# A decoder layer on one core: x over two other queues, its squares behind the operands, low halves on POOL, idle products, two more accumulator banks

## The chip, the core and the metric

The kernel runs on one core of one Trainium2 chip. A core has five engines with a queue each: TensorE (PE in the profile), VectorE (DVE), ScalarE (ACT), GpSimd (POOL) and SyncE (SP), which only issues loads. Loads and stores can be issued from SP, ACT and POOL. Each engine runs its queue strictly in order, and waits on semaphores for the others. The metric is the device time of one execution in microseconds (us), the median of the runs.

## The reference

One layer of a hybrid decoder for a prompt of 512 positions and a sample group of 8 x 8 positions, 576 columns in all, which share the weights. Only its start matters here:

```python
def rmsnorm(x, w):
    xf = x.astype(jnp.float32)
    y = xf * lax.rsqrt(jnp.mean(xf * xf, axis=-1, keepdims=True) + RMS_EPS)
    return (y * w.astype(jnp.float32)).astype(x.dtype)

def swiglu(x, w_gate, w_up, w_down):
    return (jax.nn.silu(x @ w_gate) * (x @ w_up)) @ w_down

def trunk_layer(x, conv_prev, h0, past, p):
    h = x + 0.5 * swiglu(rmsnorm(x, p['ffn1_norm']), p['ffn1_w_gate'], p['ffn1_w_up'], p['ffn1_w_down'])
    ...
```

Behind this first feed-forward step come the combined input projection, the Mamba-2 scan, attention over a paged cache with summed log forget values (cache_logf), the projections and a second feed-forward step. D_MODEL is 1024, D_FF 2816.

## The kernel before

Activations lie transposed: eight tiles hts[k] of 128 features x 576 columns. A float32 product is made of three products in float32r: both operands are split into a high half and a low half (names with hi or h, lo or l), and mm3 adds hi x hi, hi x lo and lo x hi in one PSUM bank. One accumulator holds 128 outputs x 288 columns, so each 128 outputs of a weight matrix take two accumulators (half 0 and 1) of 8 x 3 = 24 products.

At the start (from L352 on) x is loaded in five tiles xin of 128 rows, two halves each, and transposed by TensorE (tr for the prompt, mm for the sample). Norm.add makes xh on ScalarE and xl on VectorE. Weights come in stages of 512 KB (stage, L161), are copied to whi by ScalarE (L173) and the rest goes to wlo by VectorE, or POOL in a later part of the kernel (L174); whi and wlo have four buffers each. The row scales of the norm are not needed by the products: ScalarE squares the rows of xin with a sum into x0 (rsx, L391), VectorE takes the inverse root in 13 small steps, and spread (L243, L249) multiplies it out on TensorE into rbc. Only the instructions that empty an accumulator (g at L327, u at L337, both VectorE) need rbc. So TensorE can run ahead by as many accumulators as there are free banks: the tags acc and pv have two banks each.

The first feed-forward step takes for each 128 hidden features f first the gate, then the up matrix: g, its tanh on ScalarE (th, L296), s on VectorE (L297), u on VectorE, the product u times s on POOL (L338), hh on ScalarE and hl on POOL.

Beside this the setup runs: parameter loads (r, L402 to L411, transposed at L413), the page table (pcol), the convolution state (sc, transposed by TensorE at L460, copied to scT by VectorE, stored to scD), and the forget values of the cache: a gather on POOL (lg, L469), 16 scans on VectorE (pf, L474), a total (tot), one small product with the matrix page on TensorE (mm_388, L480; called the page product below), its copy st, 16 subtractions on POOL (L485) and 32 stores to pastD from ScalarE's queue (L491).

The order within each queue is set when the program is built: a scheduler replays the code with its own costs and fixes each queue's order; with soon() an instruction gets a higher priority.

Of the kernel before, what the change touches and what calls it, by code (L numbers as in the profile page):

```python
# [14 lines left out]
F32 = mybir.dt.float32  # L15
# [8 lines left out]
P = 128  # L24
# [5 lines left out]
HT = NT // 2  # L30
# [63 lines left out]
def build(ctx, tc, A, O):  # L94
    nc = tc.nc
    uid = [0]

    def tl(pool, shape, dt=F32, tag=None, bufs=None):
        uid[0] += 1
        kw = {} if bufs is None else {"bufs": bufs}  # L100
        return pool.tile(shape, dt, tag=tag, name=f"{tag}_{uid[0]}", **kw)
# [4 lines left out]
    mm = nc.tensor.matmul  # L106
    act = nc.scalar.activation
    V = nc.vector
    G = nc.gpsimd
# [10 lines left out]
    nkeep = COFF["scan"][0]  # L120
    cst = tl(constp, [P, nkeep - P], tag="cst")
    ident = tl(constp, [P, P], tag="ident")
# [9 lines left out]
    def tr():  # L132
        return bank("tr", 2)

    def sm():
        return bank("mm", 2)
# [4 lines left out]
    wide = [True, 0]  # L141

    def acc():

        wide[1] += 1
        if wide[0] and wide[1] % 2:
            return pv()[:, :HT]
        return tl(accp, [P, 512], tag="acc")[:, :HT]
# [15 lines left out]
    turn = [0]  # L164
    share = [0]

    def split(view, nk, m=P):
        hi = tl(wp, [P, nk, m], F32R, tag="whi", bufs=4)
        lo = tl(wp, [P, nk, m], F32R, tag="wlo", bufs=4)
        turn[0] += 1  # L170
        e = G if share[0] and turn[0] % share[0] == 0 else V
        with soon():
            act(hi, view, AF.Copy)  # L173
            e.tensor_tensor(lo, view, hi.bitcast(F32), ALU.subtract)  # L174
        return hi, lo
# [178 lines left out]
    with pool("h1", reuse_waits="tile") as hp:  # L354
        hts = [tl(hp, [P, NT], tag=f"h{k}") for k in range(8)]
        nrm1 = Norm(0)
        with pool("xin", side="right", reuse_waits="tile") as xi:
            su = xi
            xin = [tl(xi, [P, D], tag=f"xin{c}") for c in range(5)]
            r1 = tl(su, [8, P], tag="r1")  # L360
            nc.scalar.dma_start(out=r1, in_=A["ffn1_norm"].rearrange("o (k p) -> (o k) p", p=P))
            for half in range(2):
                d = slice(half * (D // 2), (half + 1) * (D // 2))
                for c in range(5):
                    n = P if c < 4 else NS
                    src = A["x_prompt"][0, c * P:(c + 1) * P, d] if c < 4 else A["x_sample"].rearrange("b t d -> (b t) d")[:, d]
                    (nc.sync if c % 2 == 0 else nc.scalar).dma_start(out=xin[c][:n, d], in_=src)
                if half == 0:
                    cg = Cols(A["ffn1_w_gate"][0], 0).load(0, (nc.sync, nc.scalar))
            P1 = tl(constp, [P, 66], tag="P1")  # L370
            t = tr()
            nc.tensor.transpose(t[:, :8], r1, ident[:8, :8])
            V.tensor_copy(P1[:, :8], t[:, :8])
            for k in range(8):
                t = tr()
                for c in range(4):
                    nc.tensor.transpose(t[:, c * P:(c + 1) * P], xin[c][:, k * P:(k + 1) * P], ident)
                if k % 2:
                    act(hts[k][:, :NP], t, AF.Copy)
                else:  # L380
                    V.tensor_copy(hts[k][:, :NP], t)
                t = sm()
                nc.tensor.transpose(t[:, :NS], xin[4][:NS, k * P:(k + 1) * P], ident[:NS, :NS])
                V.tensor_copy(hts[k][:, NP:], t[:, :NS])
                nrm1.add(hts[k], squares=False)
            x0 = tl(tp, [P, 5], tag="rsx", bufs=1)
            G.memset(x0, 0.0)
            for c in range(5):
                n = P if c < 4 else NS
                junk = tl(xi, [P, D], tag="junk")  # L390
                act(junk[:n], xin[c][:n], AF.Square, accum_out=x0[:n, c:c + 1])  # L391
            nc.scalar.dma_start(out=cst, in_=A["consts"][:, P:nkeep])
            V.tensor_scalar(x0, x0, 1.0 / D, EPS, ALU.mult, ALU.add)
            nrm1.r = spread(rsqrt(x0, 5), 0, tl(tp, [P, NT], tag="rbc", bufs=1))

        with pool("setup2", side="right", reuse_waits="tile") as su:
            q = nc.scalar

            r1 = tl(su, [66, P], tag="r1")

# [11 lines left out]
            t = tr()  # L412
# [7 lines left out]
            t = tr()  # L420
# [7 lines left out]
            t = tr()  # L428
# [7 lines left out]
            al = tl(constp, [48, 1], tag="al")  # L436
            V.memset(al, 0.0)
            q.dma_start(out=al[:32], in_=A["a_log"].rearrange("o h -> h o"))
            act(al, al, AF.Exp)
            V.tensor_scalar(al, al, -1.0, None, ALU.mult)  # L440

# [15 lines left out]
            for j in range(0, 24, 12):  # L457
                t = tr()
# [6 lines left out]
        with pool("lg", side="right", reuse_waits="tile") as lp:  # L465
# [4 lines left out]
                                 in_=A["cache_logf"].rearrange("o n s h -> (o n) (s h)"),  # L470
# [6 lines left out]
            t = sm()  # L477
# [46 lines left out]
    with pool("dtf", side="right", reuse_waits="tile") as dp:  # L524
# [7 lines left out]
        x0 = tl(dp, [48, NT], tag="x0")  # L532
# [7 lines left out]
        e = tl(dp, [48, NT], tag="e")  # L540
# [23 lines left out]
        for c in range(5):  # L564
            n = P if c < 4 else NS
            t = tr()
# [17 lines left out]
    with pool("att", side="right", reuse_waits="tile") as ap:  # L584
# [57 lines left out]
        for p in range(2):  # L642
            for g2 in range(0, 4, 2):
                st2 = []
                for k in range(0, 8, 4):
                    stg = tl(wp, [P, 4, 2, 2, 64], tag="stage", bufs=4)
                    for gi in range(2):
                        for e in range(2):
                            c0 = CQ + (2 * p + e) * 256 + (g2 + gi) * 64
                            nc.sync.dma_start(out=stg[:, :, gi, e, :],  # L650
                                              in_=win[k * P:(k + 4) * P, c0:c0 + 64].rearrange("(k p) c -> p k c", p=P))
                    st2.append(stg)
                for gi in range(2):
# [4 lines left out]
                    q = tl(yp, [P, NT], tag="qy", bufs=10)  # L658
# [776 lines left out]
```

## Time and profile before

| | |
|---|---|
| median of 3 runs | 1915.45 us (1914.47 to 1915.89) |
| the profiled execution | 1914.71 us, of which the span is 1912.9 us |
| mean granted TensorE clock | 0.988 |
| TensorE busy | 1840.0 us, 96% of the span |
| VectorE, ScalarE, POOL busy | 1065.6, 748.2, 652.2 us |

The span runs from the first to the last instruction in the profile. Times in the rows are microseconds from its start. In rows of single instructions stand the start, the duration, the engine (a q behind it: its queue issues a load), the source line, the operation, output <- inputs, and in brackets the engine's idle time before it and what ended that. In rows of groups stand the busy time and the mean duration in ns. In rows of waits stand the total, how often, and the longest.

### The profile page before, as it was taken

How to read it: one execution, taken by the hardware profiler on the slowest of the kernel's cores; microseconds unless marked ns; L12 is line 12 of the kernel's file. 1: busy time of each engine (PE TensorE's matmuls, PEld its weight loads, DVE VectorE, ACT ScalarE, POOL GpSimd, SP SyncE). 2: the span in 40 equal slices, each digit the busy share in tenths (PEclk: the TensorE clock that was granted, in tenths of full speed). 3: DMA queues.
4: the chain of work that ended last, by engine and by line, in shares of the span. 5: the costliest groups of instructions: out<-in, count | busy, mean ns of one | idle time of the engine just before them, and what ended most of it. 6: DMA issues, size and time to landing. Idle time of an engine off the chain costs nothing. (4 is left out here: it accounts for less than half of the span.)

```text
span 1912.9 us, 38609 instructions
## 1 busy us (share of the span) xinstructions
PE 1840.0 (96%) x15335; PEld 1731.7 (91%) x15335; DVE 1065.6 (56%) x2204; ACT 748.2 (39%) x1553; POOL 652.2 (34%) x719
## 2 busy tenths in 40 slices
PE   7999999999998999999998988989999999999999
PEld 7999999999896888888997877878889999999998
DVE  4554334445234777775729767888785544334432
ACT  4233223334222555554427455555434333223322
POOL 0433012322322344432227455675744233003310
PEclk9999999999998999999999999999999999999999
DMA  5432223234534787865465545464654332222322
GB/s 152 112 96 80 89 78 89 83 105 111 145 109 129 188 255 223 246 200 148 95 174 153 141 127 142 111 178 124 174 155 136 89 88 77 80 74 81 88 90 71
DMA packets 270841, 243.21 MB, mean 127 GB/s; under 512 B 53276, under 2 KB 243404, under 8 KB 270508
## 3 DMA queue, kind: packets, MB, share of 16 engines
q1 hardware_dynamic: 208208, 169.35, 32.4%
q10 hardware_dynamic: 53092, 36.79, 6.4%
q0 software_dynamic: 9360, 34.61, 5.6%
q8 instruction: 121, 1.98, 0.4%
q14 instruction: 60, 0.49, 0.1%
HBM read 204.97 MB, written 29.03 MB: 122 GB/s over the span
## 5 line engine op out<-in xcount | busy, mean ns | idle before, releaser
L173 ACT ACTIVATE whi<-stage 128x512 fp32r<-128x512 f32 (+2 forms) x474 | 294.6, 622 | 732.4 <-PE acc L209 640.6
L208 PE MATMUL acc<-xh,whi 128*128 128x288 f32 x1856 | 561.7, 303 | 17.8 <-DVE xr L1046 11.5
L209 PE MATMUL acc<-xl,whi 128*128 128x288 f32 x1856 | 552.6, 298 | 0.0
L210 PE MATMUL acc<-xh,wlo 128*128 128x288 f32 x1856 | 552.3, 298 | 0.0
L174 DVE TENSOR_TENSOR wlo<-stage,whi 128x512 fp32r<-128x512 f32 (+1 forms) x373 | 271.9, 729 | 263.9 <-ACT whi L173 243.8
L208 PEld LDWEIGHTS acc<-xh,whi 128*128 128x128 f32 x1856 | 351.0, 189 | 24.8 <-DVE xr L1046 11.5
L209 PEld LDWEIGHTS acc<-xl,whi 128*128 128x128 f32 x1856 | 351.3, 189 | 2.1 <-issue 1.5
L210 PEld LDWEIGHTS acc<-xh,wlo 128*128 128x128 f32 x1856 | 350.7, 189 | 2.0 <-issue 1.3
L338 POOL TENSOR_TENSOR u<-u,s 128x288 f32<-128x288 f32 x88 | 92.1, 1048 | 484.3 <-DVE u L337 427.7
L208 PE MATMUL pv<-xh,whi 128*128 128x288 f32 (+1 forms) x784 | 231.4, 296 | 2.4 <-ACT xh L220 2.2
L209 PE MATMUL pv<-xl,whi 128*128 128x288 f32 (+1 forms) x784 | 231.9, 296 | 0.6 <-DVE xl L218 0.6
L210 PE MATMUL pv<-xh,wlo 128*128 128x288 f32 (+1 forms) x784 | 231.6, 296 | 0.0
L174 POOL TENSOR_TENSOR wlo<-stage,whi 128x512 fp32r<-128x512 f32 (+1 forms) x101 | 138.2, 1368 | 269.6 <-ACT whi L173 255.6
L208 PEld LDWEIGHTS pv<-xh,whi 128*128 128x128 f32 (+1 forms) x784 | 147.3, 188 | 2.9 <-ACT xh L220 2.4
L209 PEld LDWEIGHTS pv<-xl,whi 128*128 128x128 f32 (+1 forms) x784 | 147.2, 188 | 1.2 <-DVE xl L218 0.8
L210 PEld LDWEIGHTS pv<-xh,wlo 128*128 128x128 f32 (+1 forms) x784 | 147.2, 188 | 0.2
L340 POOL TENSOR_TENSOR hl<-u,hh 128x288 fp32r<-128x288 f32 x88 | 77.5, 882 | 81.6 <-ACT hh L339 81.6
L208 PE MATMUL pv<-hh,whi 128*128 128x288 f32 x352 | 104.4, 296 | 0.0
L209 PE MATMUL pv<-hl,whi 128*128 128x288 f32 x352 | 104.3, 296 | 0.0
L208 PE MATMUL acc<-hh,whi 128*128 128x288 f32 x352 | 104.1, 296 | 0.0
L210 PE MATMUL acc<-hh,wlo 128*128 128x288 f32 x352 | 104.1, 296 | 0.0
L209 PE MATMUL acc<-hl,whi 128*128 128x288 f32 x352 | 104.1, 296 | 0.0
(335 smaller groups left out, 3470.0 us busy)
## 6 DMA issues: line engine op xcount, KB each, us to landing
stage<-in_w_in_dram SPq DMA_DIRECT2D x52, 512.0 KB
stage<-in_ffn_w_up_dram SPq DMA_DIRECT2D x44, 512.0 KB
stage<-in_ffn_w_gate_dram SPq DMA_DIRECT2D x43, 512.0 KB
stage<-in_ffn_w_down_dram SPq DMA_DIRECT2D x40, 512.0 KB
pb<-pastD SPq DMA_DIRECT2D x32, 256.0 KB
ab<-cumD SPq DMA_DIRECT2D x32, 256.0 KB
h<-in_state_ssm_dram SPq DMA_DIRECT2D x32, 256.0 KB
out_dram<-h ACTq DMA_DIRECT2D x32, 256.0 KB
```

What stands on the lines that cost most here:

```text
L173: act(hi, view, AF.Copy)
L174: e.tensor_tensor(lo, view, hi.bitcast(F32), ALU.subtract)
L208: mm(out, lhsT=hi, rhs=a, start=first and i == 0, stop=False)
L209: mm(out, lhsT=hi, rhs=b, start=False, stop=False)
L210: mm(out, lhsT=lo, rhs=a, start=False, stop=last and i == n - 1)
L338: G.tensor_tensor(u, u, sil[half], ALU.mult)
L340: G.tensor_tensor(hl[:, hs(half)], u, hh[:, hs(half)].bitcast(F32), ALU.subtract)
```

## The change

- The odd tiles of x are issued from POOL's queue in place of ScalarE's, and the first two stages of the gate matrix change their queues.
- Other small loads of the setup (the constants, eleven parameter loads, the biases) move from ScalarE's queue to POOL's; page table and convolution state stay on ScalarE's.
- The squares of x are placed behind the operands: x0 is written by VectorE from the last xl before it is cleared, so that they cannot start earlier.
- Two of the four copies of transposed tiles that ScalarE made go to VectorE.
- The first six low halves of weights are made by POOL.
- 24 products of the identity with itself stand ahead of the first transposes of x.
- The fifth and the sixth accumulator come from the tag mm, which has two banks.

```diff
     def acc():
 
         wide[1] += 1
+        if wide[1] in (5, 6):
+            return sm()[:, :HT]
         if wide[0] and wide[1] % 2:
             return pv()[:, :HT]
         return tl(accp, [P, 512], tag="acc")[:, :HT]
...
         turn[0] += 1
-        e = G if share[0] and turn[0] % share[0] == 0 else V
+        e = G if turn[0] <= 6 or share[0] and turn[0] % share[0] == 0 else V
...
-                    (nc.sync if c % 2 == 0 else nc.scalar).dma_start(out=xin[c][:n, d], in_=src)
+                    (nc.sync if c % 2 == 0 else nc.gpsimd).dma_start(out=xin[c][:n, d], in_=src)
                 if half == 0:
-                    cg = Cols(A["ffn1_w_gate"][0], 0).load(0, (nc.sync, nc.scalar))
+                    cg = Cols(A["ffn1_w_gate"][0], 0).load(0, (nc.scalar, nc.sync))
...
+            t = tr()
+            for i in range(24):
+                c = (i % 4) * P
+                mm(t[:, c:c + P], lhsT=ident, rhs=ident, start=True, stop=True)
             for k in range(8):
...
-                if k % 2:
+                if k % 4 == 3:
                     act(hts[k][:, :NP], t, AF.Copy)
...
             x0 = tl(tp, [P, 5], tag="rsx", bufs=1)
-            G.memset(x0, 0.0)
+            V.tensor_copy(x0, nrm1.xs[7][1][:, :5].bitcast(F32))
+            V.memset(x0, 0.0)
             for c in range(5):
                 n = P if c < 4 else NS
                 junk = tl(xi, [P, D], tag="junk")
                 act(junk[:n], xin[c][:n], AF.Square, accum_out=x0[:n, c:c + 1])
-            nc.scalar.dma_start(out=cst, in_=A["consts"][:, P:nkeep])
+            nc.gpsimd.dma_start(out=cst, in_=A["consts"][:, P:nkeep])
...
         with pool("setup2", side="right", reuse_waits="tile") as su:
-            q = nc.scalar
+            q = nc.gpsimd
...
             q.dma_start(out=al[:32], in_=A["a_log"].rearrange("o h -> h o"))
+            q = nc.scalar
             act(al, al, AF.Exp)
```

What the diff does not tell is how the scheduler then orders the queues. Names carry a number for each tile made; lines of the changed kernel are two to ten higher. Three places matter.

ScalarE, around the last squares (junk), first before:

```order
L379 ACTIVATE h_17_95<-tr_191 128x512
L173 ACTIVATE whi_529<-stage_523 128x512
L439 ACTIVATE al_306<-al_306 48x1
L391 ACTIVATE junk_238,rsx_230<-xin_23_104 128x1024
L220 ACTIVATE xh_200<-h_17_95,P_28_122 128x576
L220 ACTIVATE xh_213<-h_18_96,P_28_122 128x576
L173 ACTIVATE whi_595<-stage_113 128x512
L391 ACTIVATE junk_240,rsx_230<-xin_24_105 64x1024
L379 ACTIVATE h_19_97<-tr_217 128x512
L173 ACTIVATE whi_599<-stage_115 128x512
```

and then in the changed kernel, where whi_621 and whi_625 belong to the gate of f = 1, whi_691 and whi_695 to its up matrix:

```order
L175 ACTIVATE whi_621<-stage_113 128x512
L400 ACTIVATE junk_258,rsx_255<-xin_20_101 128x1024
L175 ACTIVATE whi_625<-stage_115 128x512
L400 ACTIVATE junk_260,rsx_255<-xin_21_102 128x1024
L175 ACTIVATE whi_691<-stage_547 128x512
L400 ACTIVATE junk_262,rsx_255<-xin_22_103 128x1024
L175 ACTIVATE whi_695<-stage_549 128x512
L400 ACTIVATE junk_264,rsx_255<-xin_23_104 128x1024
L400 ACTIVATE junk_266,rsx_255<-xin_24_105 64x1024
```

Before, squares stand between the operands xh; now all five stand behind them, each behind a conversion of weights for f = 1.

TensorE at the page product, before (it stands 126 products behind the second transposes of the convolution state):

```order
L208 MATMUL pv_891<-xh_226,whi_887 128x288
L209 MATMUL pv_891<-xl_227,whi_887 128x288
L210 MATMUL pv_891<-xh_226,wlo_888 128x288
L480 MATMUL mm_388<-tot_386,page_389 128x16
L208 MATMUL acc_922<-xh_135,whi_883 128x288
```

and in the changed kernel (82 products behind them):

```order
L210 MATMUL acc_877<-xh_251,whi_843 128x288
L211 MATMUL acc_877<-xl_252,whi_843 128x288
L212 MATMUL acc_877<-xh_251,wlo_844 128x288
L490 MATMUL mm_414<-tot_412,page_415 128x16
L210 MATMUL mm_629<-xh_160,whi_621 128x288
```

The fifth accumulator, mm_629 (the gate of f = 1, in the first of the two new banks), comes right behind the page product; the sixth, mm_660, follows it. At the spread TensorE has the up matrix of f = 1 (pv_699) next.

VectorE behind the page product, before (the last rows before a tanh from behind the stores is needed):

```order
L327 SCALAR_TENSOR_TENSOR g_1060<-pv_1035,rbc_259 128x288
L174 TENSOR_TENSOR wlo_1172<-stage_1023,whi_1171 128x512
L327 SCALAR_TENSOR_TENSOR g_1091<-acc_1066,rbc_259 128x288
L174 TENSOR_TENSOR wlo_1176<-stage_1025,whi_1175 128x512
L174 TENSOR_TENSOR wlo_1242<-stage_1097,whi_1241 128x512
L174 TENSOR_TENSOR wlo_1246<-stage_1099,whi_1245 128x512
```

and in the changed kernel:

```order
L176 TENSOR_TENSOR wlo_984<-stage_837,whi_983 128x512
L176 TENSOR_TENSOR wlo_1054<-stage_1049,whi_1053 128x512
L176 TENSOR_TENSOR wlo_1058<-stage_1051,whi_1057 128x512
L299 SCALAR_TENSOR_TENSOR s_687<-th_688,g_685 128x288
L329 SCALAR_TENSOR_TENSOR g_942<-pv_917,rbc_285 128x288
L299 SCALAR_TENSOR_TENSOR s_800<-th_801,g_798 128x288
L339 TENSOR_TENSOR u_872<-pv_847,rbc_285 128x288
```

The first s that needs a tanh from behind the stores now stands ahead of the g and u that empty the next accumulators; before, these came first. On ScalarE th_688 stands behind the last group of stores:

```order
L175 ACTIVATE whi_983<-stage_837 128x512
L501 DMA pastD_82<-lg_393 16x16x32 x10
L175 ACTIVATE whi_1053<-stage_1049 128x512
L501 DMA pastD_82<-lg_393 16x16x32 x3
L175 ACTIVATE whi_1057<-stage_1051 128x512
L501 DMA pastD_82<-lg_393 16x16x32 x16
L298 ACTIVATE th_688<-g_685 128x288
```

All 32 stores are ahead of it in the queue; 29 of them are shown.

## The prediction

> **What bounds the kernel now.** I read the first page, then the busy times of chosen stretches, then TensorE's waits up to 100 us, then single instructions around each wait. The first page (busy time by engine; the chain that ended last) says that one engine sets the span.
>
> ```profile
> span 1912.9 us, 38609 instructions
> PE 1840.0 (96%) x15335; PEld 1731.7 (91%) x15335; DVE 1065.6 (56%) x2204; ACT 748.2 (39%) x1553; POOL 652.2 (34%) x719
> PE acc L208 7%; PE acc L210 7%; PE acc L209 7%; PE pv L209 4%; PE pv L210 4%; PE pv L208 4%; DVE kf L1072 1%; DMA ab<-cumD 1%; PE pv L1241 1%; DVE ygl L1169 1%; DVE accs L1336 0%; ACT dk L1214 0%; PE tr L1273 0%; DVE dk L1216 0%; DMA zt<-zD 0%
> ```
>
> TensorE is busy for 1840 of 1912.9 us. So an edit pays only where it removes TensorE idling or slow TensorE, and it costs wherever TensorE comes to a wait. All the edits lie in the first 100 us. After that the two programs have the same order but for a few rows, so what is won or lost by then is carried to the end.
>
> Stretches: from:to, length, then busy time and count by engine, granted clock, DMA share, GB/s.
>
> ```profile
> 4.65:15.33 10.68, 5.64 (x22) 3.95 (x23) 2.88 (x9) 4.39 (x7) 0.00 (x0) 1.00 1.04 314
> 15.33:32.25 16.92, 16.92 (x115) 16.38 (x116) 13.34 (x34) 13.60 (x25) 0.00 (x0) 0.90 0.33 96
> 47.10:49.05 1.95, 0.04 (x1) 0.03 (x1) 1.57 (x3) 1.40 (x4) 1.95 (x3) 1.00 0.01 0
> 49.05:56.81 7.76, 7.76 (x48) 7.71 (x49) 3.11 (x6) 1.85 (x4) 5.04 (x6) 0.58 0.14 47
> 75.00:90.00 15.00, 15.00 (x115) 15.00 (x114) 5.89 (x11) 3.00 (x6) 7.84 (x17) 1.00 0.35 60
> ```
>
> At full clock a product of 288 columns costs 15.00/115 = 0.130 us. The third and the fourth row are one event: TensorE waits for the convolution state (1.95 us), and for 7.76 us behind it the granted clock is 0.58. The waits, and what opens the first product:
>
> ```profile
> PE tr L460 <- DMA sc<-in_state_conv_dram: 1.9, 1, 1.9
> PE mm L480 <- DVE tot L476: 0.7, 1, 0.7
> 14.12 0.33 ACTq L433 DMA_DIRECT2D bb<-in_dt_bias_dram  x1
> 14.50 0.77 ACT L220 ACTIVATE xh<-h,P 128x576 fp32r<-128x576 f32 x1 [2.27 <-DMA stage<-in_ffn_w_gate_dram]
> 15.33 0.40 PE L208 MATMUL pv<-xh,whi 128*128 128x288 f32 x1 [2.17 <-ACT xh L220]
> ```
>
> The change's loads aim at the 2.27 us by which ScalarE stands behind a small load; the idle products aim at the clock before 15.33; the two banks aim at the place where four accumulators are full and wait for the row scales.
>
> **The start (loads, idle products, POOL low halves).** Moving small loads off ScalarE can win its 2.27 us, and a full clock from 15.33 to 32.25 another 16.92 - 115 x 0.130 = 2.0 us: a gain of at most 4.2. Against it: the DMA share before 15.33 is 1.04, so x and the first weights come at the rate of the engines whichever queue asks. The idle products are 24 of 128 columns; in the next fence the spread's four cost 1.05 us, so 24 cost 6.3 us warm and at the 0.58 clock 10.9. They start when the norm weights are transposed, near 4.9, and TensorE takes no transpose of x before they end, between 11.2 and 15.8. Half cold, half warm they end near 13.5; transposes, copy and operand then put the first product near 15.5, where it is now. The worst case puts it 2.5 later, and low halves at POOL's price instead of VectorE's add at most 4 x (1.37 - 0.73) = 2.6:
>
> ```profile
> L174 DVE TENSOR_TENSOR wlo<-stage,whi 128x512 fp32r<-128x512 f32 (+1 forms) x373 | 271.9, 729 | 263.9 <-ACT whi L173 243.8
> L174 POOL TENSOR_TENSOR wlo<-stage,whi 128x512 fp32r<-128x512 f32 (+1 forms) x101 | 138.2, 1368 | 269.6 <-ACT whi L173 255.6
> ```
>
> The trace has no direct load from POOL's queue. Its nearest row is the gather (1.15 us of POOL, below): eight loads end near 10 us, about when the first weights land. I take 0 for the start, between -4.2 and +5.1.
>
> **First new wait: the squares.** Now (ScalarE's last square, the scale and the first and last steps of the inverse root on VectorE, a conversion, then the spread):
>
> ```profile
> 25.44 1.05 ACT L391 ACTIVATE junk<-xin 64x1024 f32<-64x1024 f32 x1
> 26.39 0.19 ACT L391 ACTIVATION_READ_ACCUMULATOR junk<-xin 64x1 f32 x1
> 26.68 0.17 DVE L393 TENSOR_SCALAR rsx<-rsx 128x5 f32<-128x5 f32 x1
> 26.89 0.17 DVE L228 TENSOR_SCALAR rsi<-rsx 128x5 int32<-128x5 int32 x1
> 27.16 0.63 ACT L173 ACTIVATE whi<-stage 128x512 fp32r<-128x512 f32 x1
> 30.24 0.17 DVE L236 SCALAR_TENSOR_TENSOR rsy<-rst,rsy 128x5 f32<-128x5 f32 x1
> 32.25 1.05 PE L243 MATMUL tr<-ident,rsy 128*128 128x128 f32 x8
> 34.49 0.40 PE L208 MATMUL pv<-xh,whi 128*128 128x288 f32 x1 [0.21 <-DVE g L327]
> ```
>
> The scales are ready at 30.41 and TensorE asks at 32.25: a slack of 1.8 us. In the new order ScalarE has the five squares between four conversions, and the last conversion (whi_695) overwrites the buffer of whi_555, which the last of the 96 products reads. So two squares cannot start before TensorE has finished, and TensorE's next row is the spread. The two new banks do not cover this: their products (mm_629 and its pair) stand behind the page product, 150 rows further. TensorE then waits for one conversion 0.63, two squares 2 x 1.24 = 2.48, scale and root of 13 steps at the 0.21 between the two first VectorE rows = 2.7, and handovers of some 0.5 (estimate): 6.3 us.
>
> Then the clock. After 1.95 us without work and 1.90 of small transposes (L460, below), 25 products took from 50.88 to 56.81, 0.237 each, against 0.130: 2.7 us lost. After waits of 0.7 and less there is no such spell. Six us of idling should bring it: the spread costs 0.8 more, and some 20 products at 0.107 extra cost 2.1. First wait: 6.3 + 0.8 + 2.1 = +9.2. A page of the Trainium skill, "TensorE: Matmul & The Clock Gate" (Part 1), says that about one idle window of 3.4 us halves the clock and as long a busy one restores it; by that figure the spell would cost 1.7 in place of 2.7 to 2.9. The 7.76 us row is longer, and I take the row.
>
> **A wait that goes: the convolution state.** Its load is issued behind a run of small ones now, and TensorE gets it at 49.05. In the new order it is issued right behind the scales' copies, and TensorE first has 52 products (6.8 us and the rest of a cold spell, some 9 us), about as long as three of these small rows need to land one after the other (scD to gather, below: 6.0). The 1.95 us and the 2.7 behind it go: -4.6 (0 at worst).
>
> **Second new wait: the page product.** The chain that leads to it:
>
> ```profile
> 49.05 1.90 PE L460 MATMUL tr<-ident,sc 24*128 24x24 f32 x24 [1.92 <-DMA sc<-in_state_conv_dram]
> 50.59 0.86 DVE L461 COPY scT<-tr 128x288 f32<-128x288 f32 x2
> 51.48 0.36 ACTq L462 DMA_DIRECT2D scD<-scT  x1
> 54.56 0.36 ACTq L467 DMA_DIRECT2D pcol<-in_page_table_dram  x1
> 57.44 1.15 POOL L469 DMA_INDIRECT lg<-in_cache_logf_dram,pcol  x1 [1.58 <-DMA page<-in_consts_dram]
> 63.82 4.53 DVE L474 TENSOR_TENSOR_SCAN pf<-cst,lg 128x128 f32<-128x128 f32 x14 [1.11 <-DMA lg<-in_cache_logf_dram,pcol]
> 69.87 0.66 DVE L174 TENSOR_TENSOR wlo<-stage,whi 128x512 fp32r<-128x512 f32 x1
> 70.45 0.76 DVE L476 COPY tot<-pf 128x16 f32<-128x16 f32 x1
> 71.26 0.40 PE L480 MATMUL mm<-tot,page 128*128 128x16 f32 x2 [0.66 <-DVE tot L476]
> ```
>
> From the state's copies (51.45) to the page product now: 19.8 us. TensorE has 126 products in that time, 16.4 us and the cold spell, and waits 0.7. In the new order 82 products stand between, 10.7 us. The chain is a little shorter, since the page table is asked for right behind scD: some 4 us to the gather, 6.4 until it lands, 16 scans at 4.53/14 = 5.2, the low half and the total 1.5: 17.1. The wait is 17.1 + 0.5 - 10.7 = 6.9, 6.2 more than now, and a cold spell of 2.7: +8.9.
>
> **Third new wait: the parked forget sums.** The 16 subtractions on POOL, ScalarE's stores of them (first and last group of 32), the first copy behind them, and a VectorE instruction that waited:
>
> ```profile
> 74.16 7.10 POOL L485 TENSOR_TENSOR lg<-pf,st 128x128 f32<-128x128 f32 x16
> 81.30 0.85 ACTq L491 DMA_DIRECT2D pastD<-lg  x2
> 96.35 3.54 ACTq L491 DMA_DIRECT2D pastD<-lg  x5
> 101.08 0.50 DVE L297 SCALAR_TENSOR_TENSOR s<-th,g 128x288 f32<-128x288 f32 x1 [3.40 <-ACT th L296]
> ```
>
> The stores hold ScalarE from 81.30 to 99.89, 18.6 us, and now nobody on TensorE's path is behind them: in 75:90 TensorE is full. In the new order the tanh th_688 is queued behind the 32 stores, VectorE's s_687 waits for it, and behind s_687 in VectorE's queue stands u_872, which frees the bank that pv_987 needs. TensorE meanwhile has only mm_629, mm_660, pv_917 and acc_948: 96 products, 12.5 us, and 2.7 cold. From the page product: its copy 0.4, subtractions 7.1, stores 18.6 less the two conversions fewer that stand among them (1.2), then tanh, s_687 and three more VectorE steps, 2.0: 26.9. Wait 26.9 - 15.2 = 11.7, and a cold spell of 2.7: +14.4. At the shortest, with stores at the 0.85/2 of their first pair, 13.6 in all, it is +10.6.
>
> **Sum.** 0 + 9.2 - 4.6 + 8.9 + 14.4 = +27.9 us on the profiled execution's 1914.71, that is 1942.6; the median of the runs is 0.74 above it, so I say 1943.
>
> The eleven parameter loads on POOL's queue (11 x 1.15 from about 34 us) end before TensorE asks for them, since it asks after the first wait; without that cover they would cost up to 5. "SBUF — State Buffer" of the Trainium skill (the trap "DVE blocks DMA") says that loads from GpSimd's queue starve while VectorE runs in a two-port mode; no row here shows such a load, and by that rule they could be some us later and TensorE would wait at L413.
>
> **Rivals.** *The stores do not reach TensorE* (chance 0.09): for it, in the trace ScalarE's block costs TensorE nothing; against it, the order of VectorE's queue. Then 9.2 - 4.6 + 8.9 = +13.5: 1929. It decides if s_687 gets its tanh before the four accumulators are full.
>
> *POOL is late at the start* (0.08): for it, POOL's low half takes twice VectorE's time and its load prices are unknown; the start then costs its +5.1 and the parameters up to 5 more: 1953. Against it, POOL is empty until 46 us in the trace.
>
> *Faster* (0.04): one mechanism, the banks cover the scales. It needs the 96 products to end later than ScalarE's squares, by at least the 5.8 us of conversion, squares and root; then the first two cold spells and waits do not arise, nor the drift of the later queues, and what is left is the start's -4.2 and the -4.6: 1907. Against it, the buffer of whi_555.
>
> *No change that a measurement can tell* (0.03; 0.2% is 3.8 us, about what one can): the start's gain and the state's wait pay for the first wait, and the other two vanish: 1915.
>
> **Numbers.** The forecast has 0.76, with its own range 1934 to 1951 from the start's bounds, the stores' shortest and the cold spells. Beside it the whole range takes in the stores' rival and POOL's: 1928 to 1954. Slower 0.93, same 0.03, faster 0.04.
>
> **What the new profile would show.** TensorE waiting some 6 us for VectorE's root at the spread and running at a low clock behind it; no wait for the convolution state; some 7 us at the page product; some 11 us, near 90 to 100, for a VectorE copy out of a bank while VectorE waits for a tanh and ScalarE issues stores; and the first product still near 15.5. I am wrong if TensorE crosses the spread without a wait, or if its queue reaches the banks' products earlier.

## The result, and the profile after

The changed kernel takes 1939.39 us (median of 4, 1934.84 to 1942.12) against 1914.96 us before (4 runs): ratio 1.0123, 95% interval 1.0106 to 1.0140. It is 24.4 us slower; 28 were forecast, and the range held the time. The first two lines of the page after answer to the first two shown of before:

```profile
span 1940.3 us, 38728 instructions
PE 1854.4 (96%) x15383; PEld 1747.2 (90%) x15383; DVE 1054.2 (54%) x2202; ACT 748.4 (39%) x1551; POOL 670.2 (35%) x743
```

The span is 27.4 us longer, and TensorE is busy for 14.4 us more. A busier TensorE here is no useful work: it is the idle products and the low clock behind the waits. What TensorE waited for behind the first 5 us and up to 215 us (engine, line, releaser: total, times, longest):

```profile
PE pv L210 <- ACT th L298: 10.1, 1, 10.1
PE tr L245 <- DVE rsy L238: 6.0, 1, 6.0
PE mm L490 <- DVE tot L486: 5.5, 1, 5.5
PE pv L210 <- ACT whi L175: 1.9, 1, 1.9
PE pv L210 <- DVE g L329: 1.6, 2, 1.0
```

The first three are the forecast waits (10.1, 6.0 and 5.5 us; 11.7, 6.3 and 6.9 were said) and the wait for the convolution state is gone. New and not forecast are 1.9 us at the start and 1.6 us in two waits for a bank to be emptied. Busy time in stretches of the changed kernel (columns as before: from:to, length, busy time and count by engine, clock, DMA share, GB/s): the start, the first wait, and the rows behind each of the three waits.

```profile
14.31:20.69 6.38, 4.48 (x24) 3.99 (x23) 4.75 (x10) 4.20 (x8) 3.79 (x4) 0.79 0.43 132
33.70:39.72 6.02, 0.06 (x1) 0.03 (x1) 3.20 (x15) 3.42 (x7) 4.13 (x9) 0.89 0.88 265
42.95:48.63 5.68, 5.68 (x23) 5.68 (x24) 2.97 (x9) 1.22 (x3) 1.61 (x3) 0.50 0.35 59
73.05:78.00 4.95, 4.95 (x21) 4.95 (x22) 0.17 (x1) 0.00 (x0) 4.04 (x12) 0.50 0.39 106
90.38:100.51 10.13, 0.00 (x0) 0.03 (x1) 1.75 (x4) 2.07 (x5) 0.72 (x1) 0.63 0.52 66
100.51:106.41 5.90, 5.90 (x24) 5.90 (x25) 4.44 (x7) 1.84 (x5) 4.49 (x7) 0.50 0.03 8
```

Read the last column but two: behind each wait the clock is 0.50, and a product takes 0.24 to 0.25 us (5.68/23, 4.95/21, 5.90/24) in place of 0.13. The second of these spells goes on to 79.40, so 23 to 25 products are slow each time. Each wait thus costs its own length and some 2.7 us more; at the first one the spread is slow too, 2.05 us in place of 1.05.

The best way to see where the time went is a ledger. TensorE runs the same 11184 products of 288 columns in both kernels; I take from TensorE's timeline when the product with a given count starts, and subtract:

| products done | before, us | changed, us | behind, us | what lies between |
|---|---|---|---|---|
| 72 | 29.09 | 30.40 | 1.3 | the start |
| 120 | 37.75 | 48.79 | 11.0 | first wait and its low clock: +9.7 |
| 216 | 57.72 | 64.22 | 6.5 | the state's wait and its low clock go: -4.5 |
| 312 | 71.51 | 87.02 | 15.5 | page product, and 1.0 for a bank: +9.0 |
| 384 | 81.15 | 109.75 | 28.6 | stores: +13.1 |
| 3840 | 555.1 | 583.7 | 28.6 | nothing |
| last | 1907.3 | 1934.5 | 27.2 | attention and scan, -1.4 |

Between the 384th and the 3840th product the difference does not move by 0.1 us. The last line does not belong to the change: between the 5520th and the 7440th product (980 to 1400 us) the difference went 29.0, 31.9, 25.6, 27.2, and in every kernel below it wanders there by 5 to 10 us (in d_00 by 20), also where TensorE's order in that part is the same. A kernel's time therefore has some microseconds in it that the edits do not set, and the ledger up to the 384th product is the finer measure. It stands for all kernels here (us behind the kernel before; each from one profiled execution, whose start alone differs by up to 1.2 us where the order is the same):

| kernel | 72 | 120 | 216 | 312 | 384 | ratio to before, interval |
|---|---|---|---|---|---|---|
| changed | 1.3 | 11.0 | 6.5 | 15.5 | 28.6 | 1.0123 (1.0106-1.0140) |
| a_nobanks | 2.0 | 11.6 | 7.1 | 6.6 | 6.5 | 1.0014 (1.0000-1.0028) |
| a_free | 6.0 | 7.1 | 2.1 | 9.2 | 21.8 | 1.0088 (1.0067-1.0109) |
| b_banks | -0.4 | -0.4 | -1.8 | 8.1 | 20.3 | 1.0091 (1.0072-1.0110) |
| a_pasthalf | 0.6 | 10.2 | 5.7 | 14.2 | 21.1 | 1.0108 (1.0088-1.0127) |
| a_pagetr | 0.6 | 8.5 | 3.9 | 6.1 | 7.5 | 1.0019 (1.0010-1.0028) |
| a_noidle | 0.7 | 9.8 | 5.2 | 14.0 | 25.3 | 1.0119 (1.0104-1.0134) |
| d_00 | 1.5 | 3.2 | 4.5 | 7.9 | 8.0 | 0.9997 (0.9986-1.0007) |
| d_01 | -0.5 | -0.4 | -4.2 | -4.2 | -4.3 | 0.9977 (0.9966-0.9989) |
| e_1 | -0.4 | -1.3 | -4.8 | -5.8 | 1.0 | 0.9982 (0.9969-0.9994) |
| d_loads | 0.3 | 5.8 | 5.8 | 5.4 | 5.3 | 1.0029 (1.0015-1.0043) |
| e_front_hf | 0.7 | -0.2 | 0.9 | 0.1 | 0.0 | 0.9995 (0.9980-1.0010) |
| b_loads | 0.9 | 1.2 | 4.8 | 3.8 | 6.0 | 1.0045 (1.0030-1.0060) |

### The profile page after: what moved, and what is told of

It reads as the page before. It is cut to its first block, busy times and chain, and to the rows that moved or that the text cites. A ratio compares the mean times of both kernels' runs of the same rounds, so it can differ in the third digit from the quotient of the medians.

```text
span 1940.3 us, 38728 instructions
## 1 busy us (share of the span) xinstructions
PE 1854.4 (96%) x15383; PEld 1747.2 (90%) x15383; DVE 1054.2 (54%) x2202; ACT 748.4 (39%) x1551; POOL 670.2 (35%) x743
## 5 line engine op out<-in xcount | busy, mean ns | idle before, releaser
L176 DVE TENSOR_TENSOR wlo<-stage,whi 128x512 fp32r<-128x512 f32 (+1 forms) x367 | 255.9, 697 | 268.0 <-ACT whi L175 252.8
L210 PEld LDWEIGHTS acc<-xh,whi 128*128 128x128 f32 x1848 | 351.1, 190 | 21.1 <-ACT tt L1071 8.3
L176 POOL TENSOR_TENSOR wlo<-stage,whi 128x512 fp32r<-128x512 f32 (+1 forms) x107 | 146.6, 1370 | 292.4 <-ACT whi L175 287.7
L210 PE MATMUL pv<-xh,whi 128*128 128x288 f32 (+1 forms) x776 | 231.2, 298 | 13.6 <-ACT th L298 10.1
L342 POOL TENSOR_TENSOR hl<-u,hh 128x288 fp32r<-128x288 f32 x88 | 77.4, 880 | 86.5 <-ACT hh L341 86.5
```

The lines of the kernel that those rows point to most:

```text
L210: mm(out, lhsT=hi, rhs=a, start=first and i == 0, stop=False)
L342: G.tensor_tensor(hl[:, hs(half)], u, hh[:, hs(half)].bitcast(F32), ALU.subtract)
```

## The experiments

**a_nobanks: the change without the two banks.**

```diff
-        if wide[1] in (5, 6):
-            return sm()[:, :HT]
```

> The changed kernel without the two more banks; all else as changed. Theory (as predicted): the second and the third new wait, at the page product and behind the stores, exist only because the fifth and sixth accumulator get a bank of their own and so move behind the page product in the order; without the banks both go. At equal counts of products the changed kernel was 1.3 us behind after 72, 11.0 after 120, 6.5 after 216, 15.5 after 312 and 28.6 after 360; what should be left is the 6.5, and nothing from 216 on: 1915 + 6 = 1921 (1917 to 1925). The wait at the spread stays at about 6 us. Rival 1: the later waits follow from the late scales (everything that reads them piles up), not from the banks: then it stays near 1939. Rival 2: the two banks do help at the spread and their loss costs there: above 1939.

1917.28 us, at the lower end of the expected 1917 to 1925. Its waits behind the start:

```profile
PE tr L243 <- DVE rsy L236: 6.0, 1, 6.0
PE pv L208 <- ACT whi L173: 1.7, 1, 1.7
PE pv L208 <- DVE g L327: 0.6, 1, 0.6
```

The 6.0 us at the spread stay to a tenth, the page product and the tanh are gone from the list, and from the 216th product on nothing is lost (7.1, 6.6, 6.5). So 22 of the 28.6 us hang on the two banks, and the first rival (later waits follow from the late scales) falls.

**b_banks: the kernel before with the two banks alone.**

```diff
+        if wide[1] in (5, 6):
+            return sm()[:, :HT]
```

> The kernel before with the two more banks alone. Theory: they alone bring the second and the third new wait: 9.0 + 13.1 = 22.1 us on 1915, so 1937 (1932 to 1941), with some 6 us at the page product and some 10 behind a tanh that stands behind the stores. Rival 1: the banks are harmless as long as the scales come early: 1915. Rival 2: the banks let TensorE run further ahead and gain the 0.7 us wait: 1913 to 1915.

1930.80 us. The two waits are there with early scales too:

```profile
PE pv L210 <- ACT th L298: 9.4, 1, 9.4
PE mm L482 <- DVE tot L478: 7.1, 1, 7.1
```

The ledger says +9.8 from 216 to 312 and +12.3 to 384, 22.1 in all as expected. The time is below the expected 1932 to 1941: the profiled span is only 15.3 us longer than before's, so some 5 us came back in the late stages.

**a_free: the change with the squares free.**

```diff
-            V.tensor_copy(x0, nrm1.xs[7][1][:, :5].bitcast(F32))
-            V.memset(x0, 0.0)
+            G.memset(x0, 0.0)
```

> The changed kernel with the squares free again (the sums are cleared on POOL as before, without the copy from the last low half of x). Theory: the first wait (6 us at the spread and the low clock behind it, 9.7 us in all between the 72nd and the 120th product) goes, the two later ones stay: 1939.4 - 9.7 = 1930 (1926 to 1934), with no wait over 1 us at the spread. Rival 1: the banks cover the scales once the squares are early, and the other waits do not arise: 1907 to 1912. Rival 2: the conversions of the next weights and not the squares' late start hold the scales: the wait stays, 1937 to 1941.

1931.52 us, inside the expected 1926 to 1934, but by two terms, one of which I had put down as zero:

```profile
PE pv L210 <- ACT th L298: 9.7, 1, 9.7
PE mm L489 <- DVE tot L485: 4.1, 1, 4.1
PE pv L210 <- ACT xh L222: 3.6, 1, 3.6
```

The spread has no wait, and from 72 to 120 only 1.1 us are lost in place of 9.7: the squares behind the operands are the first wait. But three free squares now stand on ScalarE ahead of the first operand, TensorE waits 3.6 us for it and is 6.0 behind at the 72nd product. The banks, with early scales, still bring the other two waits.

**a_pasthalf: every second store of the forget sums from SP.** The order on TensorE, VectorE and POOL is that of the changed kernel, row for row.

```diff
-                    nc.scalar.dma_start(out=pastD[b, :, q].rearrange("h g e -> g h e"), in_=lv[b * NPG:(b + 1) * NPG, :, q, :])
+                    (nc.scalar if b % 2 else nc.sync).dma_start(out=pastD[b, :, q].rearrange("h g e -> g h e"), in_=lv[b * NPG:(b + 1) * NPG, :, q, :])
```

> The changed kernel with every second of the 32 stores of the forget sums issued from SP in place of ScalarE; the order on TensorE, VectorE and POOL is the same. Theory: the third wait is the time that the stores hold ScalarE (0.35 + 0.84 + 5.37 + 2.00 + 8.00 = 16.6 us for 32, 0.52 each): 16 fewer free the tanh 8.3 us earlier, the wait falls from 10.1 to about 2, and the low clock behind it may stay (2.7) or go: 1939.4 - 8.3 = 1931 (1928 to 1932). Rival 1: the wait comes from VectorE's order alone or from the tanh's own input: no change, 1939. Rival 2: 16 stores hold SP's queue for 8 us, the next weight stages come late, and TensorE waits for a conversion instead: 1935 to 1942.

1932.66 us, just above the expected 1928 to 1932, and the interval of its ratio overlaps that of the changed kernel, so the wait and the ledger have to decide. First the chain in the changed kernel (last group of stores, the tanh behind it, VectorE's s, the product that waited), then the same place here:

```profile
90.89 8.00 ACTq L501 DMA_DIRECT2D pastD<-lg  x16
98.94 0.44 ACT L298 ACTIVATE th<-g 128x288 f32<-128x288 f32 x1 [7.44 <-DMA pastD<-lg]
99.41 0.46 DVE L299 SCALAR_TENSOR_TENSOR s<-th,g 128x288 f32<-128x288 f32 x1 [7.19 <-ACT th L298]
100.51 0.58 PE L210 MATMUL pv<-xh,whi 128*128 128x288 f32 x1 [10.14 <-ACT th L298]
```

```profile
PE pv L210 <- ACT th L298: 4.5, 1, 4.5
87.41 0.63 ACT L175 ACTIVATE whi<-stage 128x512 fp32r<-128x512 f32 x1 [5.42 <-PE acc L211]
89.02 0.63 ACT L175 ACTIVATE whi<-stage 128x512 fp32r<-128x512 f32 x1 [0.98 <-PE acc L211]
92.02 0.44 ACT L298 ACTIVATE th<-g 128x288 f32<-128x288 f32 x1 [2.37 <-DMA pastD<-lg]
```

Half the stores, and the wait falls from 10.1 to 4.5, where about 2 were expected: the stores hold the tanh. It does not fall by the whole 8.3 us, because two conversions stand between the stores in ScalarE's queue and wait for TensorE's own products (5.42 and 0.98 us idle); behind the last of them five stores remain. The low clock stays: 7.0 us are lost from 312 to 384 in place of 13.1. SP issued its 16 in 8.2 us, and no conversion came late for it.

**a_pagetr: the page product takes its bank from another tag.** One word:

```diff
-            t = sm()
+            t = tr()
             page = tl(lp, [P, P], tag="page")
```

> The changed kernel with one word changed: the page product takes its bank from the tag tr in place of mm. Theory: the fifth and the sixth accumulator stand behind the page product because they rotate through the same two banks as it does; from another tag they follow right behind the spread, and the second and third wait (9.0 + 13.1 us) go although the two banks stay: about the time of the kernel without the banks, 1917 (1914 to 1922), no wait over 3 us behind the spread, and the wait of 6 us at the spread unchanged. Rival 1: the banks as such bring the waits, by letting VectorE's order pile up: 1935 to 1941. Rival 2: the page product now meets the transposes in the banks of tr and waits there instead: 1922 to 1930.

1917.38 us, as without the banks, though the banks are in use:

```profile
PE tr L245 <- DVE rsy L238: 6.2, 1, 6.2
PE tr L490 <- issue: 2.8, 1, 2.8
PE pv L210 <- ACT whi L175: 1.6, 1, 1.6
```

In its trace the fifth accumulator follows the spread directly, with 96 products of 288 columns done (in the changed kernel 240), and the page product comes after 310 (240). This is the cause behind the second and third wait: a tag with two banks is handed out in the order of the code, and the page product is written ahead of the accumulators that rotate through the same two banks. The page product has now a wait of 2.8 us of its own.

**a_noidle: no idle products.**

```diff
-            t = tr()
-            for i in range(24):
-                c = (i % 4) * P
-                mm(t[:, c:c + P], lhsT=ident, rhs=ident, start=True, stop=True)
```

> The changed kernel without the 24 idle products. They ran from 4.77 to 11.79 us, 7.0 us, and the first product came at 14.31, 0.7 us behind the second conversion (13.5) and at once behind its operand. Theory: weights and not TensorE open the first product, so it comes 0 to 1.5 us earlier without them: 1938.5 (1936 to 1940). Rival 1: they are in the way of the transposes of x, which could start near 5 as before: 4 us earlier at the 72nd product and behind it, 1934 to 1936. Rival 2: the clock that they keep up is worth something: 1941 to 1943.

1937.91 us: 1.5 less than the changed kernel, as expected, but with overlapping intervals. By the ledger the idle products cost 0.6 us at the 72nd product and 3.3 by the 384th, and they buy nothing here; the first rival's 4 us at the start are not there.

**d_00: no banks, squares early.** The sums are cleared behind the first low half of x in place of the last.

```diff
-            V.tensor_copy(x0, nrm1.xs[7][1][:, :5].bitcast(F32))
+            V.tensor_copy(x0, nrm1.xs[0][1][:, :5].bitcast(F32))
```

> The changed kernel without the two banks (1917 so), idle products kept, with one edit more: the sums are cleared behind the first low half of x in place of the last. Theory: the wait at the spread is the late start of the squares: in the changed kernel the clear ended at 30.1 us, and five squares and four conversions followed on ScalarE without a pause, to 37.2. With the squares early the wait (6.0) and its low clock (about 3) go: 1908 to 1911, ratio 0.997 to 0.999, and no wait over 2 us at the spread. Rival 1 (as the prediction had it): the last conversion waits for the buffer that the last of the 96 products reads, and what stands behind it is late whenever the squares may start: the wait stays at 4 to 6, ratio 1.001 to 1.002. Rival 2: early squares stand ahead of the operands, the first product waits for its operand as with the squares free (3.6): ratio 0.999 to 1.001.

1910.18 us, ratio 0.9997, where 0.997 to 0.999 were expected. This time cannot be used either way: the scheduler also ordered a later stage anew. In the trace TensorE's order differs from that of before in 668 rows between 1037 and 1183 us, and there the kernel goes from 8.6 us behind to 7.6 ahead; in all other kernels the order is that of before from 136 us on, but for two neighbouring rows in e_front_hf and four in b_loads. Its trace up to the 384th product can be used:

```profile
PE mm L488 <- DVE tot L484: 2.6, 1, 2.6
PE tr L436 <- DVE P L423: 2.4, 1, 2.4
PE tr L243 <- DVE rsy L236: 1.0, 1, 1.0
```

The wait at the spread is 1.0 in place of 6.0, which decides for the squares' start. New ones of 2.6 and 2.4 stand at the page product and at the parameters' transposes.

**d_01 and e_1: versions to beat both.** d_01 is d_00 without the idle products; e_1 is the change without idle products, with early squares and the page product in tr, so that the banks are used.

> The changed kernel without the two banks and without the idle products, and with the sums cleared behind the first low half of x in place of the last. Theory: the loads over the other queues keep what they won at the convolution state (4.6 us), and with the squares early there is no wait at the spread: about 4 us below the kernel before, ratio 0.998 (0.996 to 1.000). Rival 1: as with the squares free, they stand ahead of the operands on ScalarE and the first product waits for its operand (3.6 us there, 6.0 at the 72nd product): ratio 1.000 to 1.003. Rival 2: what is won by then is lost again at the page product, whose chain sets the pace when TensorE is early (0.7 us of wait before): ratio 0.999 to 1.001.

> As the kernel without idle products whose sums are cleared behind the first low half, but with the two banks, and the page product's bank from the tag tr. Theory: now the banks do what they are for, their products stand right behind the spread, and TensorE does not stop there for the copies out of the first banks (about 1.5 us): ratio 0.997 (0.995 to 0.999), with no wait over 3 us behind 20 us. Rival 1: nothing waits at the spread by then, the banks add nothing: as the kernel without them, within 0.1%. Rival 2: waits behind the page product or the stores come back at another accumulator: ratio over 1.003.

d_01 takes 1909.03 us beside 1914.42, ratio 0.9977 (0.9966 to 0.9989), faster than both kernels and as expected. Its longest wait between 20 and 260 us:

```profile
PE pv L208 <- DVE g L327: 0.8, 1, 0.8
```

It differs from d_00 by the idle products alone, and yet it is 12.3 us ahead of d_00 at the 384th product (4.3 ahead of before in place of 8.0 behind): the waits of 2.6 and 2.4 us are not there. So what the idle products cost depends on what stands behind them. Their removal also changes the order of VectorE's and ScalarE's queues; no run separates the two.

e_1 takes 1912.74 us (0.9982), a time that cannot be told from d_01's. At 312 it is 5.8 us ahead of before, 1.6 more than d_01: that is what the banks give, about the 1.5 expected. One wait then takes it back, where none over 3 us was expected:

```profile
PE tr L486 <- issue: 4.1, 1, 4.1
71.18 0.80 DVE L482 COPY tot<-pf 128x16 f32<-128x16 f32 x1
```

It is the page product, which starts at 72.08, right behind VectorE's total: TensorE is early, and the chain of state, gather and scans sets the pace there, as the second rival in d_01's expectation has it. From 312 to 384 it loses 6.8 us, the wait and a low clock.

**e_front_hf: e_1 with that chain started early and half the stores on SP.**

```diff
-        with pool("setup2", side="right", reuse_waits="tile") as su:
+        with pool("lg", side="right", reuse_waits="tile") as lp, pool("setup2", side="right", reuse_waits="tile") as su:
+            pcol = tl(lp, [P, 1], I32, tag="pcol")
+            nc.scalar.dma_start(out=pcol, in_=A["page_table"].rearrange("b n -> (b n)").unsqueeze(1))
+            lg = tl(lp, [P, P, 16], tag="lg")
+            G.indirect_dma_start(out=lg.rearrange("p s h -> p (s h)"), out_offset=None,
+                                 in_=A["cache_logf"].rearrange("o n s h -> (o n) (s h)"),
+                                 in_offset=bass.IndirectOffsetOnAxis(ap=pcol[:, :1], axis=0))
...
-        with pool("lg", side="right", reuse_waits="tile") as lp:
```

> The kernel with the page product in another bank, no idle products and early squares (ratio 0.9982, 4.1 us of wait at the page product), in which the gather of the forget values is issued ahead of the parameter loads, its tiles lying beside those of the setup, and every second store of the forget sums goes out from SP. Theory: the page product's chain was the pace there; started some 20 us earlier it is off the path, and with half the stores no tanh comes late: the 5.8 us by which that kernel was ahead of the one before at 312 products are kept: ratio 0.997 (0.9955 to 0.998), no wait over 1 us behind the first product. Rival 1: the stores now stand ahead of tanhs that TensorE needs, and a wait of 3 to 5 us takes the place: 0.999 to 1.001. Rival 2: the gather's transfer takes the weights' time, and TensorE waits for conversions before 60 us: 0.999 to 1.002.

1911.93 us, 0.9995: not resolved from before. The page product does not wait any more, but:

```profile
PE tr L472 <- DMA sc<-in_state_conv_dram: 1.2, 1, 1.2
50.00:56.00 6.00, 6.00 (x32) 5.67 (x31) 6.00 (x15) 1.86 (x5) 2.74 (x3) 0.50 0.01 3
```

The state comes late again, and the half clock behind that wait of 1.2 us costs about 3 us in these 6 alone. The time lies within both rivals' ranges, but their waits are not there; none of the three expectations had this one. The two edits were not run apart.

**d_loads: d_01 with the old queues.**

```diff
-                    (nc.sync if c % 2 == 0 else nc.gpsimd).dma_start(out=xin[c][:n, d], in_=src)
+                    (nc.sync if c % 2 == 0 else nc.scalar).dma_start(out=xin[c][:n, d], in_=src)
...
-                    cg = Cols(A["ffn1_w_gate"][0], 0).load(0, (nc.scalar, nc.sync))
+                    cg = Cols(A["ffn1_w_gate"][0], 0).load(0, (nc.sync, nc.scalar))
...
-            nc.gpsimd.dma_start(out=cst, in_=A["consts"][:, P:nkeep])
+            nc.scalar.dma_start(out=cst, in_=A["consts"][:, P:nkeep])
...
-            q = nc.gpsimd
+            q = nc.scalar
```

> The fastest kernel so far (no two banks, no idle products, sums cleared behind the first low half: ratio 0.9977) with x, the constants, the first gate stages and the parameters loaded over their old queues again. Theory: the other queues are worth the wait for the convolution state and the low clock behind it, 1.9 + 2.7 = 4.6 us: without them the ratio is 1.000 (0.999 to 1.001), and TensorE waits 1 to 2 us for the state again. Rival 1: the gain is that of the low halves on POOL and the copies on VectorE: it stays at 0.998. Rival 2: with the small loads back on ScalarE's queue the operands or the scales come late: over 1.002.

1916.77 us, ratio 1.0029 beside 0.9977: more than the expected 1.000, and in the second rival's range. The waits for the state and at the spread come back:

```profile
PE tr L243 <- DVE rsy L236: 2.5, 1, 2.5
PE tr L463 <- DMA sc<-in_state_conv_dram: 2.2, 1, 2.2
```

The other queues are worth 9.6 us of the ledger there (5.3 against -4.3), more than the 4.6 of the state: with the old queues the scales come later too. The low halves on POOL and the copies on VectorE were not taken away alone in any run, so their part in the 5.3 us by which this kernel is behind the one before is open.

**b_loads: the kernel before with the other queues alone.** The diff of d_loads the other way round, on the kernel before.

> The kernel before with the loads alone changed: x over SP and POOL, the first gate stages exchanged, constants and parameters over POOL; squares, low halves, copies and banks as before. Theory: what the change won (the wait for the convolution state and its low clock, 4.6 us, and up to 2 of ScalarE's 2.27 behind a small load at the start) is the loads' alone: ratio 0.9975 (0.9965 to 0.999), as the fastest kernel so far (0.9977), with no wait for the state. Rival 1: the low halves on POOL and the copies on VectorE have a part in it, without them scales or operands come late: 0.999 to 1.001. Rival 2: x over POOL's queue comes later than over ScalarE's, and the first product, now at 15.3, is later by 1 to 3 us: 0.999 to 1.000.

1927.18 us beside 1917.43: ratio 1.0045, slower, which no expectation had. The state is not waited for, but the transposes ahead of it are:

```profile
PE tr L431 <- DVE P L418: 4.3, 1, 4.3
43.65 0.17 DVE L452 CAST pf<-pcol 128x8 f32<-128x8 int32 x1 [6.97 <-DMA sc<-in_state_conv_dram]
50.51 0.14 DVE L418 TENSOR_SCALAR P<-tr 128x1 f32<-128x1 f32 x1
```

VectorE stands 6.97 us at a cast that needs the page table's columns, whose loads are still on ScalarE's queue (the row names the state's load, which is on the same queue, as what came last); the copies that empty the transposes' banks (P, to 50.5) stand behind it, and TensorE waits for a bank. With that and a low clock the 4.6 us are lost and 3.6 more (1.2 at 120, 4.8 at 216). This chain is read from the trace; no run moves the page table's loads alone. In d_01 the same cast runs at 39.40, and the copies behind it cost TensorE 0.7. In the changed kernel the wait at the spread covers it: TensorE comes to these transposes only at 49.7.

## Why the prediction was right, step by step

*The start* (0 said, -4.2 to +5.1): +1.3. The idle products took 7.0 us, within the 6.3 to 10.9, and the first product came at 14.31, 1.0 us earlier and not near 15.5, but the next one waited for the conversion of the up matrix and ran at a low clock. That ScalarE's 2.27 us were spent behind a small load is not shown: the row names a stage of the gate matrix. With the loads alone moved (b_loads) the first product came at 14.08. The changed kernel:

```profile
4.77 7.02 PE L380 MATMUL tr<-ident 128*128 128x128 f32 x48
14.31 0.40 PE L210 MATMUL pv<-xh,whi 128*128 128x288 f32 x1
17.18 0.40 PE L210 MATMUL pv<-xh,whi 128*128 128x288 f32 x1 [1.90 <-ACT whi L175]
```

*First new wait* (+9.2 said, +9.7 measured): size right, and one step in it wrong. I had two squares wait behind a conversion for the buffer that the last of the 96 products reads. ScalarE did not stop there:

```profile
30.05 0.06 DVE L396 MEMSET rsx<- 128x5 f32 x1
30.14 1.06 ACT L400 ACTIVATE junk<-xin 128x1024 f32<-128x1024 f32 x1 [1.73 <-DVE rsx L396]
34.32 0.61 ACT L175 ACTIVATE whi<-stage 128x512 fp32r<-128x512 f32 x1
36.97 0.19 ACT L400 ACTIVATION_READ_ACCUMULATOR junk<-xin 64x1 f32 x1
39.72 2.05 PE L245 MATMUL tr<-ident,rsy 128*128 128x128 f32 x8 [5.96 <-DVE rsy L238]
```

It ran without a pause from the clear at 30.1 to 37.2; the conversion at 34.32 found its buffer free (TensorE's last product started at 33.47). The clear, behind the last low half of x, is the cause, as a_free and d_00 show. That 6.3 came so near to 6.0 is luck in part: ScalarE happened to reach that conversion 0.6 us after TensorE ran out (33.76), so nearly the same work was left as if it had waited. The four conversions between the squares add 4 x 0.52 (31.20 to 31.72, from one to the next square), 2.1 of the 6.0.

*The wait that goes* (-4.6 said, -4.5 measured): right in this kernel, but the reason was incomplete. It takes the loads over the other queues, and VectorE's copies behind its cast have to be done when TensorE comes; b_loads and d_00 have the first and not the second, and lose there. (In e_front_hf the cast is held for 5.2 us too, but runs at 42.7, and these transposes do not wait.)

*Second wait* (+8.9 said, +9.0 measured): right in mechanism, and in the sum with some luck. The wait was 5.5 and not 6.9, since the chain from the state's copies to the page product took 16.1 us (56.99 to 73.06) in place of 17.6. The wait of 1.0 us for a bank at 83.8, which the sum does not have, falls in the same stretch and makes up for most of it. a_pagetr adds why 82 products and not 126 stand ahead of the page product.

*Third wait* (+14.4 said, +13.1 measured): right in mechanism; the wait was 10.1 and not 11.7.

```profile
73.06 0.60 PE L490 MATMUL mm<-tot,page 128*128 128x16 f32 x2 [5.47 <-DVE tot L486]
80.18 0.35 ACTq L501 DMA_DIRECT2D pastD<-lg  x1
83.78 0.37 PE L210 MATMUL pv<-xh,whi 128*128 128x288 f32 x1 [1.01 <-DVE g L329]
```

The chain was sized well: the stores, with the conversions among them, held ScalarE from 80.18 to 98.89, 18.7 us (18.6 before), and from the page product to the product that waited (100.51) it took 27.5 us, 26.9 said. TensorE's own part was too small: it came to the wait at 90.37, 17.3 us behind the page product and not 15.2, because the wait of 1.0 us for a bank fell in between and the half clock lasted longer than the term had it (6.3 us).

*The parameter loads on POOL* (covered, up to 5 otherwise). The price was too high by two: 0.50 us each, not the gather's 1.15.

```profile
34.71 0.55 POOL L411 DMA_DIRECT2D r<-in_ffn_norm_dram  x1 [1.51 <-ACT junk L400]
40.80 0.48 POOL L433 DMA_DIRECT2D r<-in_d_skip_dram  x1 [0.23 <-DMA r<-in_ffn_norm_dram]
```

They land 4.0 to 4.9 us after issue, well ahead of 49.7. The cover was named, and it was one: without it the place costs 4.3 us (b_loads), through VectorE's queue and not through POOL's.

*The faster rival* (banks cover the scales, 1907, chance 0.04) was argued against with the wrong buffer. The real obstacles were the shared tag and the late squares; with both taken away (e_1) the banks are worth 1.6 us beside d_01, until the page product.

## What to carry to other kernels

Before a tag of PSUM banks is lent to an early accumulator, look at who else takes from it in the order of the code: one late small product can drag the accumulators, and with them the tanhs, behind it. Count what each engine's queue holds in front of the instruction that frees a bank, DMA issues included: 32 stores of 0.5 us are harmless until a tanh stands behind them. A wait often covers the next one; when a change brings a wait, the ones behind it show only when it is taken away, so undo parts both ways (from the old kernel and from the new) and compare by the count of products done.

## What the runs showed of the hardware

In the changed kernel the granted clock is 0.50 from 17.96 to 21.37, from 38.44 to 48.68, from 72.57 to 79.40 and from 93.05 to 106.70 us: one, three, two and four times 3.41 us, and the switches lie whole multiples of that apart. So a spell does not begin and end with a wait: behind the waits of 6.0, 5.5 and 10.1 us it lasted another 9.0, 6.3 and 6.2.

Much shorter waits beside small transposes brought it too: 1.95 us before (0.58 over 7.76 us), 1.90 at the start of the changed kernel (0.50 from 17.96), 1.2 in e_front_hf (0.50 for 6 us). Between large products a wait of 2.8 us brought it (a_pagetr, 0.50 from 78.57 to 81.98); one of 1.8 us (b_loads, at 77.4) and one of 1.0 us (the changed kernel, at 83.8) did not.

"TensorE: Matmul & The Clock Gate" of the Trainium skill (Part 1) says that an idle window of about 3.4 us halves the clock and a busy one restores it. The half clock and the step of 3.4 us agree; but waits shorter than that were enough here, and full clock came back 6.2 to 9.0 us behind the three long waits.
